# Second block's attention: stacked parts of queries and keys, split products, transposed results

## The chip, the cores and the metric

The kernel runs on one core of one Trainium2 chip. The metric is device time in microseconds (us), the median of three runs.

## The reference, cut to what matters

A two-stage network over 256 latent and 256 context tokens of width 1024. The stage that changes is the mixer of the second block's first layer. Its input is normed and modulated; three projections give queries, keys and values for 8 heads of 64 features, and the other half of the mixer (a long convolution, here called the hyena part) takes three more. Queries and keys are normed per head and scaled by a gain. Latent queries attend to a window of latent keys (a bias table `nabias` holds the window, with a large negative number outside) and to all context keys; context queries attend to context keys only:

```
q = rms_norm(q) * q_gain ;  k = rms_norm(k) * k_gain
latent:  s = q k^T / 8 + bias  (256 latent keys) ,  q k_ctx^T / 8  (256 context keys)
context: s = q k_ctx^T / 8     (256 context keys)
out = softmax(s) v            (per head; then side by side, times even_out, added to the stream)
```

## The kernel before, in words

Tokens stand in two segments of 256 (segment 0 latent, segment 1 context), each as two tiles of 128. Most products are done in three parts of a narrower 32-bit type (`F32R`): an operand is held as a high part H and a rest L, and `mm3` (lines 171 to 174) does H·H, H·L and L·H. `cut` (L145 to L151) makes the parts of a weight load of 128x1024: ScalarE (ACT) casts H, VectorE (DVE) subtracts for L. `split` (L176) does the same for activations. Plain `F32` products are issued in two pieces each.

The stage stands in lines 902 to 1060. Lines 912 to 931 make queries, keys and values token by token, six groups of two token tiles, 48 products of 512 columns each; queries and keys are normed and turned by four transposes per token tile into `qT` and `kT`, two heads on 128 partitions. `att2(qt, hb)` (L936 to L968) does one tile of 128 queries for four heads. Per head: one F32 score product with 64 rows (L946 or L952), for latent queries the bias is added on DVE (L947) and the other half copied by ACT (L948), DVE takes the row maximum (L956), ACT the exponential and its sum (L957), two or four transposes through the two `tp` banks and an ACT copy (L960) turn the weights, and two or four F32 products with 64 columns (L962) give the output with tokens on partitions; DVE divides by the sum (L965, L966). `heads(qt)` (L1021) later transposes and splits the result into `yH`, `yL`.

The order that the code writes: lines 1027 to 1037 alternate the hyena part's 12 `conv` products (24 products of 512 columns, then one ACT and two DVE instructions, L973 to L978) with six of the eight `att2` jobs; `spectrum(0)` (L981) comes behind the first of the last four convs, `signal(0)` (L1006) and `heads(0)`, `heads(1)` follow; then `out_proj` of segment 0 (L1059), between whose eight output tiles `rest()` puts `spectrum(1)`, the jobs 6 and 7, `heads(2)`, `heads(3)` and `signal(1)`, and then `out_proj` of segment 1.

The code's order is a priority: a planner (the tile framework) fixes each engine's order ahead of time from it and from its own estimate of when an instruction is ready, so that products of a later conv fill TensorE while an attention step waits. Tiles with one tag share a fixed number of buffers, and a new one waits until an old one is done with. Weight loads go through SP's queue; the bias tiles (L944, 16 loads of 128 KB) are issued by GpSimd (POOL), which does nothing else in this stage.

Of the kernel before, what the change touches and what calls it, by code (L numbers as in the profile page):

```python
# [10 lines left out]
F32 = mybir.dt.float32  # L11
# [62 lines left out]
def trace(tc, A, dbg=None):  # L74
# [32 lines left out]
    # ---------------------------------------------------------------- constants  # L107
# [20 lines left out]
    # ---------------------------------------------------------------- weights  # L128
# [4 lines left out]
    def queued(inst, prev):  # L133
        """Issues inst behind prev on their engine."""
# [10 lines left out]
    def cut(raw):  # L145
        """A load as its parts."""
# [6 lines left out]
    class Feed:  # L153
        """Weights in the order of their use, from the i-th load on."""
# [25 lines left out]
    # ---------------------------------------------------------------- 1/sqrt of small tiles  # L180
# [20 lines left out]
    # ---------------------------------------------------------------- modulation vectors  # L201
# [53 lines left out]
    def pump(k):  # L255
        """Emits k units behind other work: they fill what it leaves of the vector engine."""
# [36 lines left out]
    # ---------------------------------------------------------------- work put between products  # L293
# [12 lines left out]
    # ---------------------------------------------------------------- norms (features on partitions)  # L306
# [56 lines left out]
    class TwoNorms(Norm):  # L363
        """A norm with gain g, and a second norm of its result, both from sums over x: with
        v = mean(x^2) + eps, the second one's mean square + eps is (mean((x g)^2) + eps v) / v."""
# [47 lines left out]
    # ---------------------------------------------------------------- SwiGLU  # L413
# [9 lines left out]
    def up(w_gu, f, sub, hH, hL, tags):  # L423
        """One tile of hidden features of the segments in sub."""
# [22 lines left out]
    def ahead(pools, w_gu, seg, out):  # L447
        """The first tiles of hidden features of one segment, ahead of their FFN."""
# [6 lines left out]
    def ffn_steps(hp, nslot, w_gu, w_dn, keys, gate_ch, segs, norms, lead=0, done=None, pre=None):  # L455
        """One SwiGLU as steps: a tile of hidden features, or a tile of output features, each.
        With two segments the second product goes in groups of hidden tiles; the first `lead` tiles,
        and the last group of the second product, are done for one segment after the other, so that
        the norms around it overlap with products. pre: hidden tiles of the second segment at hand."""
# [442 lines left out]
    with ExitStack() as st:  # L902
# [9 lines left out]
        for i, (n, tiles) in enumerate(((0, lat), (1, lat), (0, ctx_), (1, ctx_), (2, ctx_), (2, lat))):  # L912
            out = proj_tm("even_qkv", n, tiles, ("mm", "mm") if i % 2 == 0 else ("sc", "sc"))
            tick(4)
            for ps, tt in zip(out, tiles):
                if n == 2:
                    act.copy(vt[tt], ps)
                    continue
# [114 lines left out]
        for c in range(4):  # L1033
# [3 lines left out]
            if 4 + c < 6:  # L1037
                att2(*jobs[4 + c])
# [385 lines left out]
```

## Time and profile before

| | |
|---|---|
| median of three runs | 2448.03 us (2446.39 to 2449.99) |
| the profiled execution | span 2448.3 us from first to last instruction; the page gives no other time for it |
| TensorE busy (PE) | 2409.3 us, 98% |
| DVE busy | 1690.1 us, 69% |
| ACT busy | 1011.4 us, 41% |
| POOL busy | 12.6 us |
| mean granted TensorE clock | 0.993 |

Busy times of PE count pipelined products up to a modelled end, so neighbours overlap; what one product costs in a dense stretch is read from start to start.

### The profile page before, as it was taken

The numbers are of one execution on the slowest core, as the hardware profiler recorded it, in microseconds if no ns is written. First come the engines' busy times: TensorE is split into PE (matmuls) and PEld (weight loads), VectorE is DVE, ScalarE is ACT, GpSimd is POOL, SyncE is SP. The second block draws the span as 40 slices with busy tenths as digits, with TensorE's granted clock in tenths as the row PEclk, the third lists the DMA queues.
The fourth block names the chain that finished last, engine by engine and source line by source line (L and its number), as shares of the span: only waits on it lengthen the run. The fifth ranks groups of instructions, "written<-read, shape, count | busy, mean of one in ns | idle before, by whom it ended". The sixth has DMA issues, their size and how long they took to land.

```text
span 2448.3 us, 38829 instructions
## 1 busy us (share of the span) xinstructions
PE 2409.3 (98%) x15624; PEld 2158.4 (88%) x15624; DVE 1690.1 (69%) x2957; ACT 1011.4 (41%) x1532; POOL 12.6 (1%) x27
## 2 busy tenths in 40 slices
PE   7999999999999999999999999999999999999999
PEld 4999889999998888777988888988888999999999
DVE  6889986666999588557875655886455775555554
ACT  4444575444332235555632222632222553334442
POOL 0000000000000000000000000000000000000000
PEclk8999999999999999999999999999999999999999
DMA  8887864565765455421463434564445543324554
GB/s 307 322 307 250 311 212 167 203 212 196 241 210 186 146 198 185 137 67 42 160 219 131 153 137 145 183 218 169 173 162 182 192 133 105 104 86 147 190 183 145
DMA packets 124372, 441.72 MB, mean 180 GB/s; under 512 B 13952, under 2 KB 18176, under 8 KB 124064
## 3 DMA queue, kind: packets, MB, share of 16 engines
q1 hardware_dynamic: 122928, 435.25, 51.4%
q0 software_dynamic: 1120, 3.80, 0.5%
q8 instruction: 122, 2.00, 0.3%
q14 instruction: 58, 0.48, 0.1%
q10 hardware_dynamic: 144, 0.19, 0.0%
HBM read 438.14 MB, written 1.05 MB: 179 GB/s over the span
## 4 chain that ended last, share of the span: by engine, by line
PE 90%; DVE 5%; DMA 2%; ACT 1%; issue 1%; SPq 0%; DVEq 0%; ACTq 0%
PE mm L172 15%; PE mm L173 15%; PE mm L174 15%; PE sc L174 13%; PE sc L173 13%; PE sc L172 13%; DVE wL L150 2%; DMA mraw<-in_wada_dram 1%; PE tp L574 1%; PE sm L962 1%; DVE mjunk L270 1%; PE tp L1150 1%; ACT wH L149 1%; PE sc L673 1%; DMA raw<-in_wada_sc_dram 0%
## 5 line engine op out<-in xcount | busy, mean ns | idle before, releaser
L149 ACT CAST wH<-wraw 128x1024 fp32r<-128x1024 f32 x596 | 624.6, 1049 | 1067.3 <-PE mm L173 416.3
L150 DVE TENSOR_TENSOR wL<-wraw,wH 128x1024 fp32r<-128x1024 f32 x596 | 728.0, 1223 | 396.8 <-ACT wH L149 385.3
L172 PE MATMUL mm<-yH,wH 128*128 128x256 f32 (+1 forms) x1744 | 561.9, 322 | 7.4 <-ACT wH L149 3.8
L174 PE MATMUL mm<-yH,wL 128*128 128x256 f32 (+1 forms) x1744 | 558.9, 320 | 3.6 <-DVE wL L150 3.5
L173 PE MATMUL mm<-yL,wH 128*128 128x256 f32 (+1 forms) x1744 | 560.0, 321 | 0.4 <-DVE yL L701 0.3
L174 PE MATMUL sc<-yH,wL 128*128 128x256 f32 (+1 forms) x1168 | 375.7, 322 | 2.2 <-DVE wL L150 2.2
L172 PE MATMUL sc<-yH,wH 128*128 128x256 f32 (+1 forms) x1168 | 376.5, 322 | 1.4 <-ACT yH L177 0.8
L173 PE MATMUL sc<-yL,wH 128*128 128x256 f32 (+1 forms) x1168 | 376.3, 322 | 0.0
L172 PEld LDWEIGHTS mm<-yH,wH 128*128 128x128 f32 x1744 | 330.6, 190 | 39.3 <-ACT wH L149 6.4
L174 PEld LDWEIGHTS mm<-yH,wL 128*128 128x128 f32 x1744 | 330.8, 190 | 29.0 <-DVE wL L150 4.5
L173 PEld LDWEIGHTS mm<-yL,wH 128*128 128x128 f32 x1744 | 330.6, 190 | 25.1 <-DVE yL L701 1.0
L270 DVE SCALAR_TENSOR_TENSOR mjunk<-mraw,crow_c 128x1024 bf16<-128x1024 f32 x200 | 244.1, 1220 | 23.8 <-DMA mraw<-in_wada_dram 16.9
L174 PEld LDWEIGHTS sc<-yH,wL 128*128 128x128 f32 x1168 | 221.3, 190 | 20.7 <-DVE wL L150 2.9
L172 PEld LDWEIGHTS sc<-yH,wH 128*128 128x128 f32 x1168 | 221.4, 190 | 19.6 <-ACT wH L149 1.0
L173 PEld LDWEIGHTS sc<-yL,wH 128*128 128x128 f32 x1168 | 221.6, 190 | 17.6
L174 PE MATMUL sc<-hH,wL 128*128 128x256 f32 (+1 forms) x640 | 192.9, 301 | 1.3 <-DVE wL L150 1.3
L172 PE MATMUL sc<-hH,wH 128*128 128x256 f32 (+1 forms) x640 | 194.1, 303 | 0.0
L172 PE MATMUL mm<-hH,wH 128*128 128x256 f32 (+1 forms) x640 | 194.0, 303 | 0.0
L173 PE MATMUL mm<-hL,wH 128*128 128x256 f32 (+1 forms) x640 | 193.9, 303 | 0.0
L173 PE MATMUL sc<-hL,wH 128*128 128x256 f32 (+1 forms) x640 | 193.5, 302 | 0.0
L174 PE MATMUL mm<-hH,wL 128*128 128x256 f32 (+1 forms) x640 | 192.9, 301 | 0.0
L270 DVE SCALAR_TENSOR_TENSOR mjunk<-mraw,crow_c_ctx 128x1024 bf16<-128x1024 f32 x112 | 136.8, 1222 | 4.8 <-ACT crow_c_ctx L224 2.8
(366 smaller groups left out, 3279.4 us busy)
## 6 DMA issues: line engine op xcount, KB each, us to landing
mraw<-in_wmod_dram SPq DMA_DIRECT2D x144, 512.0 KB, 4.6
wraw<-in_fa_gu_dram SPq DMA_DIRECT2D x114, 512.0 KB, 3.6
wraw<-in_fb_gu_dram SPq DMA_DIRECT2D x94, 512.0 KB, 3.3
wraw<-in_w_gu_dram SPq DMA_DIRECT2D x88, 512.0 KB, 3.7
wraw<-in_fa_dn_dram SPq DMA_DIRECT2D x60, 512.0 KB, 3.5
mraw<-in_wada_dram SPq DMA_DIRECT2D x56, 512.0 KB, 5.4
wraw<-in_fb_dn_dram SPq DMA_DIRECT2D x52, 512.0 KB, 3.3
wraw<-in_w_dn_dram SPq DMA_DIRECT2D x44, 512.0 KB, 4.0
```

Of the source, the lines that this page charges most:

```text
L149: act.copy(H, raw)
L150: vec.tensor_tensor(L, raw, f32(H), op=OP.subtract)
L172: pe.matmul(ps, aH, bH, start=start, stop=False)
L173: pe.matmul(ps, aH, bL, start=False, stop=False)
L174: pe.matmul(ps, aL, bH, start=False, stop=stop)
L270: queued(vec.scalar_tensor_tensor(junk, raw, 1.0, row_of(c), op0=OP.mult, op1=OP.mult, accum_out=mod[key][:, ch * 8 + j:ch * 8 + j + 1]), ...
L574: pe.transpose(pt[:, j * P:j * P + P], src(j), ident)
L673: pe.matmul(scp[j], csil[:, k:k + 1], raw[:, j * 512:j * 512 + 512], start=k == 0, stop=k == ND - 1)
L962: pe.matmul(po[:, (h % 4) * 64:(h % 4) * 64 + 64], pT[:, i, :], vt[kt][:, h * 64:h * 64 + 64], start=i == 0, stop=i == n - 1)
L1150: pe.matmul(ps[:, c], kT[:, j, jt * P:jt * P + P], qT[:, j, :], start=j == 0, stop=j == 1)
```

## The change

- Queries and keys stay token-major after their norm (`qkn`); the 32 transposes that turned them move into `att2_open(hp)`, once per pair of heads: eight transposes into both `tp` banks, then for each of the two heads H and L of the query (gain and 1/8 folded in) on the two halves of 128 partitions (`qq`), H of the key on both halves (`kH`), L of the key on one half with zeros on the other (`kL`), and H and L of the values side by side (`vv`; the subtraction on POOL).
- A score is two F32R products of 128 rows: `qq` with `kH`, `qq` with `kL`.
- `att2(h, seg)` does one head for both query tiles of a segment. For segment 1 the maximum and the exponential read the bank directly. The weights are divided by their sum before the transposes, on POOL; behind the transposes they are split into H (ACT) and L (DVE).
- The output has features on partitions: `vv` is the stationary operand, H and L of the weights are the moving ones (256 columns), and the two halves of the result are added (ACT copy, DVE add). `heads` has no transposes any more.
- Order: pairs of heads, segment 0 then 1, two (head, segment) steps between two convs; 14 of 16 steps stand ahead of the last four convs, the last two (heads 6 and 7 of segment 1) in `rest()`, ahead of `spectrum(1)`.
- Buffers: `spectrum` now takes its four work tiles from the two buffers of `a2pH` and the two of `a2pL`; `hyx0` takes the buffer of the token-major queries; `hy_b` has one buffer instead of two.

The diff also drops comments, which is left out here, as is the body of the old `att2`, which stands above.

```diff
@@ -902,70 +902,104 @@
     with ExitStack() as st:
         mp = pool("mix2", stack=st)
         wk = pool("mix2w", 2, stack=st)
-        hyx0 = tl(mp, [P, 4, 512], F32, "hyx0")
         hyz = tl(mp, [P, 4, 512], F32, "hyz")
         dft = tl(mp, [P, 8, P], F32, "dft")
         nc.sync.dma_start(dft, A["dft"].rearrange("p (n q) -> p n q", n=8))
-        qkT = [tl(mp, [P, 4, 512], F32, f"qk2T{i}") for i in range(2)]
-        vt = [tl(mp, [P, 512], F32, f"v2_{tt}") for tt in range(4)]
+        qkn = [tl(mp, [P, 4, 512], F32, f"qk2n{i}", 1) for i in range(2)]
+        vt = tl(mp, [P, 4, 512], F32, "v2")
+        pos = tl(mp, [P, 4, 512], F32, "at2")
         lat, ctx_ = (0, 1), (2, 3)
         for i, (n, tiles) in enumerate(((0, lat), (1, lat), (0, ctx_), (1, ctx_), (2, ctx_), (2, lat))):
             out = proj_tm("even_qkv", n, tiles, ("mm", "mm") if i % 2 == 0 else ("sc", "sc"))
             tick(4)
             for ps, tt in zip(out, tiles):
                 if n == 2:
-                    act.copy(vt[tt], ps)
+                    act.copy(vt[:, tt, :], ps)
                     continue
                 sq = tl(tpool, [P, 512], F32, "sg", 2)
                 act.activation(sq, ps, AF.Square)
                 ss = tl(spool, [P, 8], F32, "qss")
                 vec.tensor_reduce(ss, sq.rearrange("p (h e) -> p h e", h=8), AX, OP.add)
                 rs = mean_rsqrt(ss, 8, 64)
-                qn = tl(tpool, [P, 512], F32, "hf", 2)
-                vec.tensor_tensor(qn.rearrange("p (h e) -> p h e", h=8),
+                vec.tensor_tensor(qkn[n][:, tt, :].rearrange("p (h e) -> p h e", h=8),
                                   ps.rearrange("p (h e) -> p h e", h=8),
                                   rs.rearrange("p (h o) -> p h o", o=1).to_broadcast([P, 8, 64]), op=OP.mult)
-                tk = slice(tt * P, tt * P + P)
-                gcol = V("q_gain" if n == 0 else "k_gain")
-                transpose4(lambda j: qn[:, j * P:j * P + P],
-                           lambda pt: act.activation(qkT[n][:, :, tk], pt, AF.Identity, scale=gcol))
-        qT, kT = qkT
-        pos = [tl(mp, [P, 512], F32, f"at2_{qt}") for qt in range(4)]
-        rsum = tl(mp, [P, 4, 8], F32, "rsum2")
-        def att2(qt, hb):
-            po = bank("sm", [P, T])
-            for h in range(hb * 4, hb * 4 + 4):
-                rows = slice((h % 2) * 64, (h % 2) * 64 + 64)
-                qs = qT[rows, h // 2, qt * P:qt * P + P]
+        qg8 = tl(mp, [P, 1], F32, "qg8")
+        vec.tensor_scalar(qg8, V("q_gain"), 0.125, None, op0=OP.mult)
+        halves = (slice(0, 64), slice(64, P))
+        kL = [tl(mp, [P, 512], F32R, f"kL{e}") for e in range(2)]
+        for e in range(2):
+            vec.memset(f32(kL[e][halves[1 - e], :]), 0.0)
+            act.copy(kL[e][halves[1 - e], :], f32(kL[e][halves[1 - e], :]))
+        def att2_open(hp):
+            out = []
+            qt, kt = bank("tp"), bank("tp")
+            for n, pt in enumerate((qt, kt)):
+                for tt in range(4):
+                    pe.transpose(pt[:, tt * P:tt * P + P], qkn[n][:, tt, hp * P:hp * P + P], ident)
+            for e in range(2):
+                own, other = halves[e], halves[1 - e]
+                gq, gk = qg8[own, :], V("k_gain")[own, :]
+                qq = tl(wk, [P, 512], F32R, "qq", 2)
+                kH = tl(wk, [P, 512], F32R, "kH", 2)
+                act.activation(qq[own, :], qt[own, :], AF.Identity, scale=gq)
+                vec.scalar_tensor_tensor(qq[other, :], qt[own, :], gq, f32(qq[own, :]), op0=OP.mult, op1=OP.subtract)
+                act.activation(kH[own, :], kt[own, :], AF.Identity, scale=gk)
+                act.copy(kH[other, :], f32(kH[own, :]))
+                vec.scalar_tensor_tensor(kL[e][own, :], kt[own, :], gk, f32(kH[own, :]), op0=OP.mult, op1=OP.subtract)
+                h = 2 * hp + e
+                vv = tl(wk, [P, 4, 2, 64], F32R, "vv", 2)
+                src = vt[:, :, h * 64:h * 64 + 64]
+                act.copy(vv[:, :, e, :], src)
+                nc.gpsimd.tensor_tensor(vv[:, :, 1 - e, :], src, f32(vv[:, :, e, :]), op=OP.subtract)
+                out.append((qq, kH, kL[e], vv))
+            return out
+        def att2(h, seg, parts):
+            qq, kH, kL, vv = parts
+            nk, k0 = (512, 0) if seg == 0 else (T, T)
+            n = nk // P
+            pH = tl(wk, [P, 4, T], F32R, "a2pH", 2)
+            pL = tl(wk, [P, 4, T], F32R, "a2pL", 2)
+            for i in range(2):
+                qt = 2 * seg + i
+                tk = slice(qt * P, qt * P + P)
                 s = tl(wk, [P, 512], F32, "a2s", 4)
...
+                ps = bank("sc", [P, nk])
+                pe.matmul(ps, qq[:, tk], kH[:, k0:], start=True, stop=False)
+                pe.matmul(ps, qq[:, tk], kL[:, k0:], start=False, stop=True)
+                if seg == 0:
                     bt = tl(tpool, [P, T], F32, "hn", 3)
                     nc.gpsimd.dma_start(bt, A["nabias"][h, qt])
+                    vec.tensor_tensor(s[:, :T], ps[:, :T], bt, op=OP.add)
+                    act.copy(s[:, T:], ps[:, T:])
+                raw = s if seg == 0 else ps
                 nmx = tl(spool, [P, 1], F32, "nmx")
+                vec.tensor_reduce(nmx, raw[:, :nk], AX, OP.max, negate=True)
+                rsum = tl(spool, [P, 1], F32, "rsum2")
+                act.activation(s[:, :nk], raw[:, :nk], AF.Exp, bias=nmx, accum_out=rsum)
+                rin = tl(spool, [P, 1], F32, "sm_rin1")
+                vec.reciprocal(rin, rsum)
+                nc.gpsimd.tensor_scalar(s[:, :nk], s[:, :nk], rin, None, op0=OP.mult)
+                o = slice(i * P, i * P + P)
+                transpose4(lambda j: s[:, j * P:j * P + P], lambda pt: split(pH[:, :n, o], pL[:, :n, o], pt), n)
+            po = bank("sm", [P, T])
+            for j in range(n):
+                for x in (pH, pL):
+                    pe.matmul(po, vv[:, k0 // P + j, :, :], x[:, j, :], start=j == 0 and x is pH,
+                              stop=j == n - 1 and x is pL)
+            own, other = (slice(0, 64), slice(64, P)) if h % 2 == 0 else (slice(64, P), slice(0, 64))
+            low = tl(tpool, [P, T], F32, "sq", 4)
+            act.copy(low[own, :], po[other, :])
+            vec.tensor_tensor(pos[own, h // 2, seg * T:seg * T + T], po[own, :], low[own, :], op=OP.add)
         def conv(n, dst):
             ps = bank("mm")
@@ -979,16 +1013,16 @@
                                      op0=OP.mult, op1=OP.add)
         def spectrum(s):
-            """Transform of z, and its product with the filter's."""
-            zt = tl(wk, [P, 2, 512], F32, "zt", 1)
+            zt = tl(wk, [P, 2, 512], F32, "a2pH", 2)
             for par in range(2):
                 tk = slice(s * T + par, s * T + T, 2)
                 transpose4(lambda j: hyz[:, j, tk],
                            lambda pt: act.copy(zt[:, par, :].rearrange("p (n q) -> p n q", n=4), pt))
-            zr = tl(wk, [P, 2, 512], F32, "zr", 1)
-            zi = tl(wk, [P, 2, 512], F32, "zi", 1)
+            zr = tl(wk, [P, 2, 512], F32, "a2pL", 2)
+            zi = tl(wk, [P, 2, 512], F32, "a2pL", 2)
             half_spectra(dft, zt, zt, zr, zi, ("mm", "mm"))
-            yr = tl(wk, [P, 2, 512], F32, "yr", 1)
+            yr = tl(wk, [P, 2, 512], F32, "a2pH", 2)
             vec.tensor_tensor(yr, zr, specA, op=OP.mult)
             for i in range(2):
                 u = tl(tpool, [P, 512], F32, "sg", 2)
@@ -1018,39 +1052,45 @@
                 vec.tensor_tensor(o, o, hyx0[:, c, sl], op=OP.mult)
                 split(yH[:, 4 + c, sl], yL[:, 4 + c, sl], o)
-        def heads(qt):
-            tk = slice(qt * P, qt * P + P)
-            transpose4(lambda j: pos[qt][:, j * P:j * P + P], lambda pt: split(yH[:, :4, tk], yL[:, :4, tk], pt))
+        def heads(s):
+            sl = slice(s * T, s * T + T)
+            split(yH[:, :4, sl], yL[:, :4, sl], pos[:, :, sl])
         hyfeed = Feed("even_hy", 0)
-        jobs = [(qt, hb) for qt in range(4) for hb in range(2)]
+        todo = [(2 * hp + e, seg) for hp in range(4) for seg in range(2) for e in range(2)]
+        held = {}
+        def attend(n):
+            for _ in range(n):
+                h, seg = todo.pop(0)
+                if h % 2 == 0 and seg == 0:
+                    held[h // 2] = att2_open(h // 2)
+                att2(h, seg, held[h // 2][h % 2])
         for c in range(4):
             conv(4 + c, hyz[:, c, :])
-            att2(*jobs[c])
-            b = tl(wk, [P, 512], F32, "hy_b", 2)
+            attend(2)
+            b = tl(wk, [P, 512], F32, "hy_b", 1)
             conv(8 + c, b)
             vec.tensor_tensor(hyz[:, c, :], b, hyz[:, c, :], op=OP.mult)
+            if c < 3:
+                attend(2)
+        hyx0 = tl(mp, [P, 4, 512], F32, "qk2n0", 1)
         for c in range(4):
             conv(c, hyx0[:, c, :])
             if c == 0:
                 Y = spectrum(0)
-            if 4 + c < 6:
-                att2(*jobs[4 + c])
         signal(0, Y)
         heads(0)
-        heads(1)
         def rest():
-            """What the second segment lacks, between the products of the first."""
+            for _ in range(2):
+                attend(1)
+                yield
             Y = spectrum(1)
             yield
-            att2(*jobs[6])
-            yield
-            att2(*jobs[7])
-            yield
-            heads(2)
-            yield
-            heads(3)
+            heads(1)
             yield
             signal(1, Y)
             yield
```

## Rows read from the trace of the kernel before

**Rows 1.** The page: engines over the whole span, and the chain that ended last.

```profile
PE 2409.3 (98%) x15624; PEld 2158.4 (88%) x15624; DVE 1690.1 (69%) x2957; ACT 1011.4 (41%) x1532; POOL 12.6 (1%) x27
...
PE 90%; DVE 5%; DMA 2%; ACT 1%; issue 1%; SPq 0%; DVEq 0%; ACTq 0%
```

**Rows 2.** Windows of the stage: stretch, length, busy time (instructions) per engine, clock, DMA.

```profile
948.80:1009.50 60.70, 60.00 (x273) 47.97 (x272) 45.06 (x139) 32.96 (x42) 1.64 (x3) 1.00 0.54 181
1015.40:1097.90 82.50, 81.63 (x417) 59.82 (x417) 42.00 (x68) 40.85 (x82) 6.95 (x13) 1.00 0.23 73
1097.90:1132.20 34.30, 32.94 (x170) 24.09 (x168) 25.16 (x39) 18.78 (x46) 0.00 (x0) 1.00 0.13 47
1132.20:1178.00 45.80, 44.91 (x315) 38.19 (x316) 38.05 (x73) 23.35 (x57) 0.00 (x0) 1.00 0.23 77
```

**Rows 3.** Lines by shape, 936 to 1260 us, PE: the scores (busy, mean ns).

```profile
L946 PE MATMUL sc<-qk2T,qk2T 64*128 64x512 f32 x32 | 13.5, 641 | 0.9 <-ACT a2s L948 0.9
L952 PE MATMUL sc<-qk2T,qk2T 64*128 64x256 f32 x32 | 9.1, 428 | 0.0
```

**Rows 4.** Timeline of PE, 1015 to 1139 us: start, length, what.

```profile
1015.44 1.13 PE L946 MATMUL sc<-qk2T,qk2T 64*128 64x512 f32 x4
...
1090.65 1.07 PE L962 MATMUL sm<-v,a2pT 128*128 128x64 f32 x8
1091.53 0.47 PE L172 MATMUL mm<-yH,wH 128*128 128x512 f32 x1
...
1092.07 0.40 PE L174 MATMUL mm<-yH,wL 128*128 128x512 f32 x1
1092.31 0.39 PE L172 MATMUL mm<-yH,wH 128*128 128x512 f32 x1
...
1097.90 1.11 PE L574 MATMUL tp<-ident,hyz 128*128 128x128 f32 x8
...
1129.46 0.38 PE L1012 MATMUL mm<-dft,zt 128*128 128x128 f32 x2
...
1138.36 0.28 PE L172 MATMUL sc<-yH,wH 128*128 128x256 f32 x1
1138.48 0.28 PE L173 MATMUL sc<-yL,wH 128*128 128x256 f32 x1
```

**Rows 5.** Lines by shape, 936 to 1260 us, ACT.

```profile
L957 ACT ACTIVATE a2s<-a2s,nmx 128x512 f32<-128x512 f32 x16 | 11.5, 720 | 2.6 <-DVE nmx L956 2.6
L960 ACT COPY a2pT<-tp 128x512 f32<-128x512 f32 x16 | 9.4, 585 | 10.2 <-PE tp L574 9.6
L957 ACT ACTIVATE a2s<-a2s,nmx 128x256 f32<-128x256 f32 x16 | 8.1, 506 | 3.1 <-DVE nmx L956 3.1
L957 ACT ACTIVATION_READ_ACCUMULATOR a2s<-a2s,nmx 128x1 f32 x32 | 6.1, 189 | 0.0
L948 ACT ACTIVATE a2s<-sc 128x256 f32<-128x256 f32 x16 | 5.5, 371 | 6.4 <-DVE a2s L947 6.4
L931 ACT ACTIVATE qk2T<-tp,vecs 128x512 f32<-128x512 f32 x8 | 5.5, 690 | 3.6 <-PE tp L574 3.6
```

**Rows 6.** The same view, DVE and POOL.

```profile
L956 DVE TENSOR_REDUCE nmx<-a2s 128x1 f32<-128x512 f32 x16 | 10.6, 681 | 5.1 <-ACT a2s L948 5.1
L947 DVE SCALAR_TENSOR_TENSOR a2s<-sc,hn 128x256 f32<-128x256 f32 x16 | 6.7, 419 | 3.4 <-PE sc L946 3.2
L976 DVE SCALAR_TENSOR_TENSOR hyx<-mm,vecs,hyx 128x510 f32<-128x510 f32 x4 | 3.0, 742 | 0.0
L178 DVE TENSOR_TENSOR yL<-tp,yH 128x512 fp32r<-128x512 f32 x4 | 2.7, 684 | 0.0
```

**Rows 7.** Lines over the whole span, POOL: its one large elementwise instruction.

```profile
L743 POOL TENSOR_SCALAR_AFFINE_SELECT wst<-wst 128x1024 f32<-128x1024 f32 x1 | 1.1, 1087 | 9.6 <-DMA wst<-in_wsT_dram 9.6
```

**Rows 8.** Timeline of DVE, 1100 to 1119 us: inside and at the end of the first spectrum.

```profile
1109.50 1.29 DVE L995 TENSOR_TENSOR sg<-zi,specB 128x512 f32<-128x512 f32 x2
...
1117.46 0.69 DVE L1003 TENSOR_TENSOR yr<-zi 128x512 f32<-128x512 f32 x1
```

More of the change, by code (lines that the diff above doesn't have):

```diff
@@ L941, in att2 @@
+        def att2(h, seg, parts):
[7 more added lines that the diff above has]
+                tk = slice(qt * P, qt * P + P)
                 s = tl(wk, [P, 512], F32, "a2s", 4)
-                if qt < 2:
+                ps = bank("sc", [P, nk])
+                pe.matmul(ps, qq[:, tk], kH[:, k0:], start=True, stop=False)
+                pe.matmul(ps, qq[:, tk], kL[:, k0:], start=False, stop=True)
+                if seg == 0:
@@ L943, in att2 @@
                     bt = tl(tpool, [P, T], F32, "hn", 3)
                     nc.gpsimd.dma_start(bt, A["nabias"][h, qt])
-                    ps = bank("sc")
-                    pe.matmul(ps, qs, kT[rows, h // 2, :], start=True, stop=True)
-                    vec.scalar_tensor_tensor(s[:, :T], ps[:, :T], 0.125, bt, op0=OP.mult, op1=OP.add)
-                    act.activation(s[:, T:], ps[:, T:], AF.Copy, scale=0.125)
-                    nk, kts = 512, (0, 1, 2, 3)
-                else:
-                    ps = bank("sc", [P, T])
-                    pe.matmul(ps, qs, kT[rows, h // 2, T:], start=True, stop=True)
-                    act.activation(s[:, :T], ps, AF.Copy, scale=0.125)
-                    nk, kts = T, (2, 3)
@@ L955, in att2 @@
-                nmx = tl(spool, [P, 1], F32, "nmx")
-                vec.tensor_reduce(nmx, s[:, :nk], AX, OP.max, negate=True)
-                act.activation(s[:, :nk], s[:, :nk], AF.Exp, bias=nmx, accum_out=rsum[:, qt, h:h + 1])
-                pT = tl(wk, [P, 4, P], F32, "a2pT", 2)
-                n = len(kts)
-                transpose4(lambda j: s[:, j * P:j * P + P], lambda pt: act.copy(pT[:, :n, :], pt), n)
-                for i, kt in enumerate(kts):
-                    pe.matmul(po[:, (h % 4) * 64:(h % 4) * 64 + 64], pT[:, i, :], vt[kt][:, h * 64:h * 64 + 64],
-                              start=i == 0, stop=i == n - 1)
@@ L964, in att2 @@
-            rin = tl(spool, [P, 4], F32, "sm_rin4")
-            vec.reciprocal(rin, rsum[:, qt, hb * 4:hb * 4 + 4])
-            vec.tensor_tensor(pos[qt][:, hb * T:hb * T + T].rearrange("p (h e) -> p h e", h=4),
-                              po.rearrange("p (h e) -> p h e", h=4),
-                              rin.rearrange("p (h o) -> p h o", o=1).to_broadcast([P, 4, 64]), op=OP.mult)
+                    vec.tensor_tensor(s[:, :T], ps[:, :T], bt, op=OP.add)
+                    act.copy(s[:, T:], ps[:, T:])
```

## Prediction, made before the changed kernel was run

> **What bounds the kernel now.** I read the page first: PE is busy 98% of the span and 90% of the chain that ended last is PE [rows 1]. So time is saved where PE is given less to do, as long as nothing else becomes late. Next come the windows of the stage [rows 2]: the q, k, v projections (948.8 to 1009.5), the stretch from the first score product to the last product of the hyena part's z (1015.4 to 1097.9, "the first part"), the rest up to the output product, and the output product of segment 0 with what is put between its tiles. PE is full in each, at the full clock of 2.4 GHz (1.00). DVE and ACT are about half used in the first part (42.0 and 40.9 of 82.5 us), but DVE is at 38.1 of 45.8 in the last window. The reader should see that PE work taken out is worth its time only while these two stay below PE. The lines by shape and the timeline give prices.
>
> **PE, part by part.** Pitches from start to start [rows 4]: a 512-column product 0.235 us (1092.07 to 1092.31), a 256-column one 0.12, a transpose 0.14 (eight in 1.11), one head's eight value pieces 0.88, so 0.11 each.
> - Projections: 32 transposes of queries and keys leave this window: -4.5 us. They reappear in the first part as 4 openings of 8.
> - First part before: 7 convs x 24 x 0.235 = 39.5, score pieces 13.5 [rows 3], 64 transposes 9.0, 128 value pieces 14.1: 76.1. The window took 82.5, a factor 1.08 for switching between kinds.
> - First part after: the same convs 39.5; openings 4.5; 32 score products of 512 columns for the 16 latent (head, tile) steps 7.5; 24 of 256 columns for 12 context ones 2.9; 88 transposes 12.3; 88 value products of 256 columns 10.6: 77.3, times 1.08 = 84. This stretch does not shrink, since it now also holds six heads of segment 1 and the openings.
> - Behind it: jobs 4 and 5 are gone from the next stretch: 16 score pieces (half of the 9.1 of [rows 3], 4.6), 16 transposes 2.2, 32 value pieces 3.5, with 8 output transposes 1.1: -11.4.
> - The last window loses the same 11.4 for jobs 6 and 7 with their output transposes and gets 3.1 (two heads: 8 score products 1.0, 8 transposes 1.1, 8 value products 1.0): -8.3.
>
> All together PE has about 22.7 us less: -4.5 + 1.5 - 11.4 - 8.3.
>
> **ACT in the first part.** Before: 40.9, of which attention is 11.5 + 9.4 + 5.5 + 16 x 0.19 = 29.4 [rows 5]; 11.5 is left for convs and casts. After: a latent step is 0.72 + 0.19 + 0.37 + 0.585 = 1.87, times 16 = 29.8; a context step 0.51 + 0.19 + 0.37 = 1.07, times 12 = 12.8; 14 copies of half the output 5.2; per head in an opening 0.69 + 0.69 (as L931 [rows 5]), a copy between the halves 0.59 and the value cast 0.37, 8 x 2.34 = 18.7. Sum 66.5 + 11.5 = 78.
>
> **DVE in the first part.** Before 42.0; attention was 10.6 + 6.7 + about 2.4 = 19.7 [rows 6], so 22.3 stays. After: a latent step 0.42 + 0.68 + 0.2 + 0.68 = 1.98, times 16 = 31.7; a context step 0.41 + 0.2 + 0.42 = 1.03, times 12 = 12.4; 14 additions 5.9; 16 subtractions in the openings at the conv's 0.74 [rows 6], 11.8. Sum 61.8 + 22.3 = 84. Two instructions of 0.69 in a row take 1.29 [rows 8], 0.09 less than their durations, so some 124 more instructions cost about 74 when they stand dense. I take 78, the middle.
>
> **POOL** has only DMA issues here. It gets 32 multiplications and 8 subtractions; the trace holds one large elementwise instruction, 1.09 us for 1024 elements [rows 7], so 0.55 and 0.27 by length. Bounds: hidden (0), or 1.09 each on the path. Its bias DMAs, unchanged in number, now stand in one queue with multiplications that wait for a DVE reciprocal; three buffers cover that, and if they don't, a latent step waits for its bias. The transposes wait for POOL, and behind them in PE's fixed order stand conv products. SP's queue gets nothing; weight casts stand behind more ACT and DVE work, and if late, conv products wait.
>
> **The sum.** In the first part PE 84, DVE 78, ACT 78: three engines that feed each other in a chain, where before only PE was full. 84 is the lower bound. The upper one is a serial reading: `att2_open` holds both `tp` banks and the double buffers of `qq`, `kH`, `vv`, so a pair begins when the one before has let go: 5.8 for the opening (1.1 of transposes and two times 2.34 of ACT), about 10 for the first latent chain (score to addition 7.5 and 13 hand-offs of an estimated 0.2), 5.6 for three more at ACT's 1.87, 5 for the tail of segment 1: 26.4, three times, and 21 for the last pair, which leaves its segment 1 to later: 100; with POOL at its upper price 107. I take 94, 12% above PE's 84, nearer to the lower end because conv work fills gaps on all three. In the spare 10 us PE runs the next convs ahead.
>
> The first spectrum starts when this part ends. Before, from its transposes at 1097.9 to its last DVE instruction at 1118.1 [rows 4, 8], it took 20.2; PE then needed until 1129.5 for convs and jobs 4 and 5 before `signal(0)` [rows 4]. Now its buffers are the attention's, so it cannot start sooner, and `signal(0)` starts at 1015.4 + 94 + 20.2 = 1129.6: nothing gained there; the 11.4 us of PE are eaten by the spectrum's chain. In the last window DVE's work is unchanged (two heads' context steps 4.1 + 0.8 and a split 1.2 against eight maxima, four divisions and two splits, about 6), so 38.1 is its floor against PE's 45.8 - 8.3 = 37.5; with both full I take 42: -4. Total: -4.5 + 0 - 4 = -8.5 on the profiled 2448.3, which is 0.3 above the median: **2439.5 us**. What a measurement of this kernel can tell from no change is about 0.2%, 4.9 us.
>
> **Rivals.**
> 1. PE stays the only bound and all 22.7 us are seen: 2426. For it: DVE and ACT sit below PE in each window; the planner fills gaps well today (1.4 us of 34.3 idle [rows 2]). Against: three engines within 10% of each other. Chance 0.15.
> 2. POOL and DVE hinder each other. In this kernel POOL never works beside DVE, so no row speaks against it. 14 of the 15 us of POOL's new work (about 1.07 ns an element [rows 7]) lie in the first part; if DVE stands still for that long, it has 92, and with the same 12% the part takes 103: +0.6, 2448.6. The Trainium skill has such a rule in "SBUF — State Buffer", section "SBUF: two separate sides": GpSimd and a DVE instruction with two SBUF inputs take a shared port pair in turns, and the loser waits for the whole instruction. Chance 0.24, no change.
> 3. Slower: the shared buffers make pairs serial. Place: `tp`, `qq`, `vv` between pairs, and `a2pH`/`a2pL` between attention and spectrum. Price: a first part of 107 puts `signal(0)` 13 later, and in the last window heads 6 and 7 wait for `signal(0)`, `spectrum(1)` for them, which takes the 4 back: -4.5 + 13 = +8.6, 2457. It decides from a first part of about 102 on, where the sum is zero. For it: before, spectrum had its own tiles and the query and key tiles were whole. Against: score products let `qq` go early. Chance 0.21.
> That the change doesn't make the score products cheaper is unlikely, and gets no chance of its own: two of 512 columns at 0.235 are 0.47 per head, where the F32 ones took 13.5 us for 16, 0.84 each [rows 3], and 0.57 each at best, side by side in two halves of the rows (four pieces in 1.13 [rows 4]).
>
> **How the numbers follow.** My case (2432 to 2443) has 0.40, rival 1 0.15: faster 0.55. Rival 2 is no change, 0.24; rival 3 slower, 0.21. The range runs from near rival 1 to near rival 3, 2427 to 2455, and leaves out about 0.2; the forecast's own range is 2432 to 2443.
>
> **What would show it.** Right: the projections' window about 4 us shorter; the first part 90 to 98 us with ACT and DVE near 80% or more; PE idle before `signal(0)` with DVE in the spectrum; value products at 0.12. Wrong: a first part at 84 and PE full (rival 1); durations of two-input DVE instructions grown next to POOL's (rival 2); openings that wait for the pair before, with PE, DVE and ACT idle at once (rival 3). A granted clock below 1.00 in the spectrum's stretch, which no window shows today, would add to it.

## The result: slower, and the profile after

The changed kernel takes 2467.2 us (median; 2464.24 to 2469.64) against 2449.01 us for the kernel before in the same comparison: a ratio of 1.0074, interval 1.0062 to 1.0085. The forecast was 2439.5, its range 2427 to 2455. The profiled executions are 2467.9 and 2448.3 us long. The page of the changed kernel, engines over the whole span, answers to [rows 1]:

```profile
PE 2402.0 (97%) x15512; PEld 2162.1 (88%) x15512; DVE 1726.5 (70%) x3038; ACT 1026.7 (42%) x1556; POOL 64.6 (3%) x67
```

PE was given less to do, as planned, and the kernel is longer. So waits are to be looked for, and the windows say where. The four stretches are those of [rows 2], cut at the same events in both kernels: the projections; the first score product to the first transpose of the hyena part's z ("first part"); from there to `signal(0)`; from there to the first product of the norm that closes segment 0 (L343). Columns are as in [rows 2].

```profile
948.80:1005.00 56.20, 56.20 (x243) 45.61 (x242) 45.51 (x141) 28.34 (x35) 1.64 (x3) 1.00 0.59 197
1015.60:1122.80 107.20, 87.21 (x428) 66.87 (x429) 77.61 (x156) 70.48 (x156) 51.33 (x47) 0.91 0.19 59
1122.80:1148.70 25.90, 24.09 (x98) 17.19 (x97) 19.70 (x26) 7.79 (x11) 0.00 (x0) 0.97 0.12 41
1148.70:1208.00 59.30, 50.79 (x344) 46.14 (x343) 44.78 (x86) 25.59 (x49) 5.13 (x4) 0.88 0.23 76
```

The last two stretches of the kernel before, cut in this way, are:

```profile
1097.90:1129.50 31.60, 31.02 (x154) 22.41 (x153) 23.46 (x37) 16.18 (x43) 0.00 (x0) 1.00 0.14 51
1129.50:1186.00 56.50, 54.83 (x398) 47.60 (x396) 45.39 (x88) 31.98 (x70) 0.00 (x0) 1.00 0.25 85
```

Nearly all of the loss stands in one place: the first part went from 82.5 to 107.2 us, the spectrum's stretch gave 5.7 back, the last one lost 2.8. In the first part PE is idle for 20 us, and the mean granted clock is 0.91, so PE ran some of it at the lower level, 1.2 GHz; before it was 1.00. The waits of the changed kernel between 1015 and 1125 us (who waits <- for whom: us in total, times, longest) name the cause:

```profile
PEld tp L574 <- POOL a2s L990: 20.8, 22, 2.6
ACT a2pH L177 <- PE tp L574: 19.8, 19, 2.2
DVE a2pL L178 <- ACT a2pH L177: 16.8, 20, 2.0
POOL a2s L990 <- DVE sm_rin L989: 15.2, 10, 3.8
PE tp L574 <- POOL a2s L990: 13.8, 19, 1.9
```

L990 is the division by the sum, a multiplication on POOL. The transposes of the weights wait for it (one stall can stand in both of PE's lines, so they are not to be added), and ACT and DVE, which split what the transposes give, wait for PE in turn. POOL itself waits for the reciprocal (L989): it is a link in a chain, not a full engine. The lines of POOL by shape, 1011.7 to 1215 us:

```profile
L990 POOL TENSOR_SCALAR a2s<-a2s,sm_rin 128x512 f32<-128x512 f32 x16 | 25.7, 1611 | 6.2 <-DVE sm_rin L989 5.0 <-ACT a2s L982 1.1
L990 POOL TENSOR_SCALAR a2s<-a2s,sm_rin 128x256 f32<-128x256 f32 x16 | 19.2, 1206 | 54.4 <-DVE sm_rin L989 51.7 <-PE sc L977 2.8
```

The reader is to see the means: 1.61 us for 512 elements and 1.21 for 256, where [rows 7] had 1.09 for 1024, for another instruction. The timeline shows the link at work (start, length, what, in brackets the idle time before it and who ended it):

```profile
1066.55 0.17 DVE L989 RECIPROCAL sm_rin<-rsum 128x1 f32<-128x1 f32 x1
...
1066.63 1.23 DVE L150 TENSOR_TENSOR wL<-wraw,wH 128x1024 fp32r<-128x1024 f32 x1
...
1066.88 1.76 POOL L990 TENSOR_SCALAR a2s<-a2s,sm_rin 128x256 f32<-128x256 f32 x1 [1.83 <-DVE sm_rin L989]
...
1068.70 0.44 PE L574 MATMUL tp<-ident,a2s 128*128 128x128 f32 x2 [0.94 <-POOL a2s L990]
...
1068.89 0.48 PE L173 MATMUL mm<-yL,wH 128*128 128x512 f32 x1
...
1070.71 0.92 POOL L990 TENSOR_SCALAR a2s<-a2s,sm_rin 128x256 f32<-128x256 f32 x1
```

The reciprocal ends at 1066.72; the transposes start at 1068.70, 0.06 after POOL has ended. The conv product at 1068.89 needs nothing of this, but it stands behind the transposes in PE's fixed order, and so it waits too.

### The profile page after: what moved, and what is told of

Its sections match the earlier page's. It is cut to its first block, busy times and chain, and to the rows that moved or that the text cites. A ratio compares the mean times of both kernels' runs of the same rounds, so it can differ in the third digit from the quotient of the medians.

```text
span 2467.9 us, 38788 instructions
## 1 busy us (share of the span) xinstructions
PE 2402.0 (97%) x15512; PEld 2162.1 (88%) x15512; DVE 1726.5 (70%) x3038; ACT 1026.7 (42%) x1556; POOL 64.6 (3%) x67
## 4 chain that ended last, share of the span: by engine, by line
PE 50%; DVE 2%; ACT 0%; issue 0%; POOL 0%; ACTq 0%; DVEq 0%; POOLq 0%
PE mm L172 8%; PE mm L173 8%; PE mm L174 8%; PE sc L174 8%; PE sc L173 8%; PE sc L172 8%; PE tp L1190 1%; DVE wL L150 0%; PE sm L174 0%; PE sm L173 0%; PE sm L172 0%; PE tp L574 0%; PE mm L1046 0%; ACT wH L149 0%; PE sm L343 0%
## 5 line engine op out<-in xcount | busy, mean ns | idle before, releaser
L150 DVE TENSOR_TENSOR wL<-wraw,wH 128x1024 fp32r<-128x1024 f32 x596 | 728.7, 1224 | 378.6 <-ACT wH L149 367.3
L172 PE MATMUL mm<-yH,wH 128*128 128x256 f32 (+1 forms) x1744 | 562.4, 323 | 8.0 <-ACT wH L149 3.8
L172 PE MATMUL sc<-yH,wH 128*128 128x256 f32 (+1 forms) x1168 | 378.8, 324 | 1.5 <-ACT a2s L987 1.4
L172 PEld LDWEIGHTS mm<-yH,wH 128*128 128x128 f32 x1744 | 332.0, 190 | 34.2 <-ACT yH L358 4.2
L172 PEld LDWEIGHTS sc<-yH,wH 128*128 128x128 f32 x1168 | 223.1, 191 | 20.1 <-ACT a2s L987 1.6
L172 PE MATMUL sc<-hH,wH 128*128 128x256 f32 (+1 forms) x640 | 194.0, 303 | 0.0
L172 PE MATMUL mm<-hH,wH 128*128 128x256 f32 (+1 forms) x640 | 193.9, 303 | 0.0
```

What stands on the lines that cost most here:

```text
L150: vec.tensor_tensor(L, raw, f32(H), op=OP.subtract)
L172: pe.matmul(ps, aH, bH, start=start, stop=False)
```

## The experiments

All are edits of the changed kernel. Ratios are to the kernel before, from the same comparison.

**The multiplication on DVE** (`e1_mul_dve`).

```diff
-                nc.gpsimd.tensor_scalar(s[:, :nk], s[:, :nk], rin, None, op0=OP.mult)
+                vec.tensor_scalar(s[:, :nk], s[:, :nk], rin, None, op0=OP.mult)
```

> Edit: the multiplication of the softmax weights by 1/sum runs on DVE instead of POOL. Theory A (the multiplication on POOL, 1.61 us for 512 and 1.21 for 256 columns, is what the transposes and behind them all of TensorE wait for): the first part goes from 107 us to 93-99, waits of TensorE on the multiplication below 10 us, total 2450-2458. Theory B (shared buffers make the steps serial): the first part stays within 3 us of 107, total 2462-2470. Theory C (DVE and ACT are simply full): total not below 2464, since DVE gets 28 more instructions there.

Measured: 2454.35 us, ratio 1.0031 (1.0019 to 1.0042). On DVE one multiplication takes 0.33 to 0.75 us. The first part:

```profile
1012.80:1109.60 96.80, 86.12 (x428) 67.03 (x429) 86.07 (x184) 69.45 (x156) 14.38 (x19) 0.93 0.20 66
```

It is 10.4 us shorter than with POOL, although DVE now has 86 us of work in it. Over the whole kernel, PE's products wait 3.3 us for the multiplication, where they waited 15.5 for POOL's.

**The multiplication taken out** (`e2_no_mul`).

```diff
-                nc.gpsimd.tensor_scalar(s[:, :nk], s[:, :nk], rin, None, op0=OP.mult)
```

> Edit: the multiplication by 1/sum is left out (the weights are not divided by their sum, everything else stands). A: the whole price of the step goes: first part 88-97, total 2444-2454. B: first part above 103, total above 2461. C: in between, 2455-2462, since only POOL work is taken away and POOL is at 51 of 111 us.

Measured: 2437.76 us, ratio 0.9961 (0.9946 to 0.9976). Between the ratios of the two kernels, 1.0074 and 0.9961, lie 27.7 us: this one line costs more than the whole loss. The first part, the spectrum's stretch and the last one:

```profile
1009.90:1094.40 84.50, 80.36 (x431) 63.29 (x431) 74.75 (x155) 70.21 (x157) 12.52 (x19) 1.00 0.21 69
1094.40:1120.00 25.60, 24.06 (x96) 17.77 (x96) 20.74 (x27) 7.21 (x10) 0.00 (x0) 0.94 0.18 62
1120.00:1176.60 56.60, 49.54 (x344) 45.42 (x343) 44.76 (x86) 25.38 (x49) 0.00 (x0) 0.91 0.24 83
```

84.5 us at a clock of 1.00 is close to the 84 that the prediction counted as PE's floor, with DVE at 75 and ACT at 70 us beside it.

**The spectrum in tiles of its own** (`e4_spec_bufs`): rival 3's shared `a2pH` and `a2pL`. The keys' token-major tile and the values' tile, both read to the end by then, hold the spectrum.

```diff
-        vt = tl(mp, [P, 4, 512], F32, "v2")
+        vt = tl(mp, [P, 4, 512], F32, "v2", 1)
...
-            zt = tl(wk, [P, 2, 512], F32, "a2pH", 2)
+            zy = tl(mp, [P, 4, 512], F32, "qk2n1", 1)
+            zt, yr = zy[:, :2, :], zy[:, 2:, :]
...
-            zr = tl(wk, [P, 2, 512], F32, "a2pL", 2)
-            zi = tl(wk, [P, 2, 512], F32, "a2pL", 2)
-            half_spectra(dft, zt, zt, zr, zi, ("mm", "mm"))
-            yr = tl(wk, [P, 2, 512], F32, "a2pH", 2)
+            zz = tl(mp, [P, 4, 512], F32, "v2", 1)
+            zr, zi = zz[:, :2, :], zz[:, 2:, :]
+            half_spectra(dft, zt, zt, zr, zi, ("mm", "mm"))
```

> Edit: spectrum takes its four work tiles from the buffers of the token-major keys and of the values (free after the last opening) instead of those of the attention's split weights; POOL keeps its multiplication. A: the first part stays at 107; only the steps of heads 6 and 7 of segment 1 come sooner, total 2461-2467. B: spectrum no longer waits for the last attention step nor that step for signal(0): signal(0) starts 5-15 us sooner, total 2450-2460.

Measured: 2465.47 us, ratio 1.0075 (1.006 to 1.0091). The first part is still 105.9 us (1015.7 to 1121.6), and `signal(0)` comes 25.9 after it. These buffers hold nothing up.

**The multiplication twice** (`e5_mul_twice`).

```diff
                 nc.gpsimd.tensor_scalar(s[:, :nk], s[:, :nk], rin, None, op0=OP.mult)
+                nc.gpsimd.tensor_scalar(s[:, :nk], s[:, :nk], 1.0, None, op0=OP.mult)
```

> Edit: a second multiplication on POOL, by 1.0, behind the first. A: POOL's chain grows by another 1.6 or 0.9 us per step, 28 steps in the first part, of which half or more is seen: total 2485-2510. B: hidden behind waits for buffers, total 2466-2474. C: hidden likewise, 2466-2476.

Measured: 2485.91 us, ratio 1.0157 (1.0142 to 1.0172), 20.3 us above the changed kernel by the ratios. The first part is 126.7 us at a granted clock of 0.81. POOL's lines by shape, 1011 to 1210 us:

```profile
L990 POOL TENSOR_SCALAR a2s<-a2s,sm_rin 128x512 f32<-128x512 f32 x16 | 25.0, 1565 | 5.2 <-DVE sm_rin L989 5.0
L991 POOL TENSOR_SCALAR a2s<-a2s 128x512 f32<-128x512 f32 x16 | 24.2, 1515 | 0.8
L990 POOL TENSOR_SCALAR a2s<-a2s,sm_rin 128x256 f32<-128x256 f32 x16 | 18.6, 1168 | 44.0 <-DVE sm_rin L989 44.0
L991 POOL TENSOR_SCALAR a2s<-a2s 128x256 f32<-128x256 f32 x16 | 14.5, 912 | 0.4
```

The second multiplication has 38.7 us of its own, and the time grows by 20: the chain has some slack, but not enough for the second copy. The granted clock fell too, from 0.91 to 0.81, so not all of the 20 us need be waiting. POOL is busy for 84.9 of the 126.7 us, so it isn't full even here.

**POOL as busy as ever, but nobody waits for it** (`f1_mul_aside`).

```diff
-                nc.gpsimd.tensor_scalar(s[:, :nk], s[:, :nk], rin, None, op0=OP.mult)
+                jk = tl(wk, [P, 512], BF16, "jk", 1)
+                nc.gpsimd.tensor_scalar(jk[:, :nk], s[:, :nk], rin, None, op0=OP.mult)
```

> Edit: POOL multiplies as in the changed kernel, but into a tile that nobody reads; the transposes take the weights not divided by their sum (the division is left out of the output). A (what costs is that the transposes wait for POOL): as without the multiplication, 2437-2443, first part 84-88, though POOL is as busy as in the changed kernel. Rival 2 (POOL beside DVE slows DVE, or the queue of bias loads behind POOL's work is late): 2452-2467.

Measured: 2440.85 us, ratio 0.997 (0.996 to 0.998). POOL's lines, 1011 to 1150 us:

```profile
L991 POOL TENSOR_SCALAR jk<-a2s,sm_rin 128x512 bf16<-128x512 f32 x16 | 25.6, 1602 | 8.8 <-DVE sm_rin L989 8.2
L991 POOL TENSOR_SCALAR jk<-a2s,sm_rin 128x256 bf16<-128x256 f32 x16 | 17.9, 1118 | 39.1 <-DVE sm_rin L989 36.6 <-ACT a2pH L177 1.5
```

And the first part in its window:

```profile
1013.70:1098.10 84.40, 80.17 (x431) 63.12 (x431) 74.67 (x155) 70.29 (x157) 49.80 (x47) 1.00 0.22 70
```

POOL does 49.8 us of work beside DVE, and the first part is 84.4 as with none of it. So the loss is the wait, not the load on a shared resource: rival 2's mechanism costs this stage nothing that can be measured.

**The division behind the products** (`e6_div_behind`). It computes all that is asked: the output, with queries along its columns, is multiplied by 1/sum, which two F32 products with an identity spread over the partitions, into the other half of the bank.

```diff
+            rins = []
...
-                nc.gpsimd.tensor_scalar(s[:, :nk], s[:, :nk], rin, None, op0=OP.mult)
+                rins.append(rin)
...
-            po = bank("sm", [P, T])
+            pb = bank("sm")
+            po, rb = pb[:, :T], pb[:, T:]
...
+            for i in range(2):
+                pe.matmul(rb[:, i * P:i * P + P], rins[i].to_broadcast([P, P]), ident, start=True, stop=True)
             low = tl(tpool, [P, T], F32, "sq", 4)
             act.copy(low[own, :], po[other, :])
-            vec.tensor_tensor(pos[own, h // 2, seg * T:seg * T + T], po[own, :], low[own, :], op=OP.add)
+            vec.tensor_tensor(low[own, :], po[own, :], low[own, :], op=OP.add)
+            vec.tensor_tensor(pos[own, h // 2, seg * T:seg * T + T], low[own, :], rb[own, :], op=OP.mult)
```

> Edit: no multiplication ahead of the transposes; 1/sum is spread over the partitions by two products per head and segment behind the value products, and DVE multiplies the output by it. A (what costs is a slow step in the chain ahead of the transposes, not the division as such): near the run without the division (2437.8), plus at most 7 us of TensorE (64 pieces of 0.11) and some DVE: 2438-2446, first part 84-91. Rival D (ACT, DVE and TensorE are so full that each added instruction costs its length): 2446-2454, as with the multiplication on DVE (2454.4).

Measured: 2447.13 us, ratio 0.9994 (0.9985 to 1.0003): above the 2438 to 2446 of reading A, and inside the range of rival D, for which each added instruction costs its length. The first part is 90.1 us (1015.0 to 1105.1), 5.6 more than without a division. It has 50 more PE instructions than `e2_no_mul`, an estimated 5.5 us at 0.11 each, and 6.3 us more of DVE. Either would account for the 5.6 us; which of the two does is not shown.

**The same, with the transforms in other banks** (`e7_sc_banks`).

```diff
-            half_spectra(dft, zt, zt, zr, zi, ("mm", "mm"))
+            half_spectra(dft, zt, zt, zr, zi, ("sc", "sc"))
```

> Edit: as e6, and the spectrum's transforms use the two sc banks instead of the two mm banks. E (from the first spectrum transpose to signal(0) it is 26 us because the transforms hold the convs' banks and TensorE has nothing else to do): that stretch falls to 20-22, total 4-6 below e6. Rival (it is the chain of the spectrum on DVE): the stretch stays above 24, total within 2 of e6.

Measured: 2440.01 us, ratio 0.9963 (0.9949 to 0.9977). It asks why the spectrum's stretch took 25.9 us after, where 20.2 were forecast. PE's timeline of the changed kernel in that stretch:

```profile
1125.99 2.11 PE L584 MATMUL mm<-a2pH,dft 128*128 128x512 f32 x4
1128.78 1.13 PE L584 MATMUL mm<-a2pH,dft 128*128 128x512 f32 x2 [0.67 <-ACT hf L586]
1130.10 1.13 PE L584 MATMUL mm<-a2pH,dft 128*128 128x512 f32 x2 [0.20 <-DVE a2pL L589]
1131.90 0.50 PE L172 MATMUL mm<-yH,wH 128*128 128x512 f32 x1 [0.67 <-ACT hf L586]
```

The transforms (L584) sit in the two `mm` banks, which the conv products need; between them PE is idle, for 1.5 us in all, and the convs come only behind the last of them: 72 products, 16.9 us at 0.235 each. With the transforms in `sc`, the timeline of `e7_sc_banks` reads:

```profile
1106.16 2.12 PE L584 MATMUL sc<-a2pH,dft 128*128 128x512 f32 x4
...
1108.58 0.40 PE L172 MATMUL mm<-yH,wH 128*128 128x512 f32 x1
...
1109.05 1.03 PE L584 MATMUL sc<-a2pH,dft 128*128 128x512 f32 x2
...
1110.15 0.40 PE L172 MATMUL mm<-yH,wH 128*128 128x512 f32 x1
1110.39 1.02 PE L584 MATMUL sc<-a2pH,dft 128*128 128x512 f32 x2
```

Convs now stand between the transforms, and the stretch fell to 19.6 us from the 26.1 of `e6_div_behind`:

```profile
1102.80:1122.40 19.60, 18.44 (x84) 13.39 (x82) 17.91 (x25) 9.27 (x13) 0.00 (x0) 1.00 0.08 27
```

The idle time is the smaller part of this gain. The lines by shape count the conv products that are left for the stretch; L172 is one in three of them, first `e6_div_behind` (1105.1 to 1131.2 us), then `e7_sc_banks` (1102.8 to 1122.4):

```profile
L172 PE MATMUL mm<-yH,wH 128*128 128x512 f32 x24 | 9.6, 399 | 0.7 <-ACT hf L586 0.7
...
L172 PE MATMUL mm<-yH,wH 128*128 128x512 f32 x16 | 6.3, 395 | 0.0
```

Of all three lines 72 products became 50. The others now run in the first part, which holds 202 conv products instead of 181 and is no longer for it (89.8 us against 90.1): with `mm` left to the convs, they fill gaps there.

**Own tiles for the spectrum, and `spectrum(1)` earlier** (`e9_own_bufs`): `e6_div_behind` with the tiles of `e4_spec_bufs` and the last two attention steps behind `spectrum(1)`.

```diff
         def rest():
+            Y = spectrum(1)
+            yield
             for _ in range(2):
                 attend(1)
                 yield
-            Y = spectrum(1)
-            yield
```

> Edit: as e6, and spectrum has work tiles of its own (the buffers of the token-major keys and of the values), so spectrum(1) is put ahead of the last two attention steps again, as it was before. B (buffers shared by spectrum and attention hold the last window): signal(0) to the norm behind segment 0 (57-59 us) falls by 4-9, total 4-9 below e6. Rival: the window is filled by DVE, total within 2 of e6.

Measured: 2444.9 us, ratio 0.9989 (0.998 to 0.9997). The last stretch is 52.9 us (1127.3 to 1180.2) against 54.4. The step is 2 us where 4 to 9 were expected, and the intervals of the two kernels overlap.

**Both together** (`e8_both`): the edits of `e7_sc_banks` and `e9_own_bufs`.

> Edit: e7 and e9 together. B and E: the gains add, 8-14 below e6, so 2426-2434, below the kernel before by 14-22. Rivals: within 3 of e6.

Measured: 2443.27 us, ratio 0.9983 (0.9974 to 0.9992): a miss. The spectrum's stretch is short (19.6 us), but the last one has grown to 57.5. The gains don't add up.

**1/sum spread by one transpose per tile** (`f2_div_turned`): `e7_sc_banks` with one transpose where an F32 product stood.

```diff
-                pe.matmul(rb[:, i * P:i * P + P], rins[i].to_broadcast([P, P]), ident, start=True, stop=True)
+                pe.transpose(rb[:, i * P:i * P + P], rins[i].to_broadcast([P, P]), ident)
```

> Edit: as the run with the division behind the products and the sc banks, but 1/sum is spread by one transpose per tile instead of a product of two pieces: 32 x (0.22 - 0.14) = 2.6 us of TensorE less. If TensorE bounds the first part: 1-3 us below 2440; if DVE does: within 1.5 us.

Measured: 2444.79 us, ratio 0.9985 (0.9976 to 0.9994): a miss, no gain over `e7_sc_banks`. The first part is 92.3 us, not shorter than 89.8, but it holds 218 conv products, 16 more. PE then has too few left for the spectrum's stretch and waits for DVE at its end (PE, 1117 to 1126 us):

```profile
1120.17 0.28 PE L978 MATMUL sc<-kL,qq 128*128 128x256 f32 x1
1125.26 1.01 PE L1051 MATMUL mm<-dft,a2pH 128*128 128x128 f32 x3 [4.80 <-DVE qk2n L1017]
```

L1051 is the first product of `signal(0)`. So the stretch stays at 19.4 us, the length of the spectrum's chain, and the products that ran ahead gain nothing.

**That, with the spectrum in tiles of its own** (`f3_turned_bufs`), the order of `rest()` as in the change.

> Edit: as f2, and spectrum with work tiles of its own (buffers of the token-major keys and of the values), the order of rest() left as in the changed kernel. B: the last window no longer waits for signal(0) to give up its buffers, 2-5 us below f2. Rival: within 1.5 us of f2.

Measured: 2445.64 us, ratio 0.9987 (0.9978 to 0.9996). The buffers make no difference here either.

**The best version again** (`g1_best_again`): `e7_sc_banks` timed again, unchanged.

> The kernel with the division behind the products and the transforms in the sc banks again, in more rounds. If its gain is real: 2437-2443, ratio to the kernel before 0.995-0.998, interval below 1. If it was the luck of few runs: 2443-2447, as its neighbours f2 and f3.

Measured: 2441.21 us, ratio 0.9975 (0.9966 to 0.9985). By the ratios it is 0.25% faster than the kernel before, about 6 us (the medians of this comparison, 2441.21 and 2444.94, are 3.7 apart), and about 24 us faster than the changed one.

## Why the prediction was wrong

**The step that failed** is POOL's multiplication, its price and its place. The price was "0.55 and 0.27 by length", from the row of another instruction [rows 7], with 1.09 as upper bound; it measured 1.61 and 1.21, above the bound for either length. And the 94 us chosen for the first part have no term for the wait of the transposes. With that wait the first part took 107.2 us, without it 84.5 (`e2_no_mul`) and 84.4 (`f1_mul_aside`). That conv products cannot pass a late transpose was written down ("behind them in PE's fixed order stand conv products"); with the price so small it was given no weight. The text also gave 100 us for a serial reading and 107 "with POOL at its upper price", and chose 94 because conv work would fill the gaps. That it came out at 107.2 is chance: with the multiplication gone, nothing of the serial reading is left.

What the price alone is worth is not shown. On DVE the multiplication took 0.33 to 0.75 us, near the price assumed, and the first part was still 96.8 us; but there DVE had 11.3 us more work than in `e2_no_mul`.

Every stretch against the forecast, from the profiles. The projections and the first opening run up to the first score, which came 1.0 us earlier than before, counted from the norm's closing product ahead of the stage (L329, 912.1 and 913.3 us).

| | forecast | after | without the multiplication |
|---|---|---|---|
| up to the first score | -4.5 | -1.0 | -1.1 |
| first part | +11.5 | +24.7 | +2.0 |
| up to `signal(0)` | -11.4 | -5.7 | -6.0 |
| up to the norm's end, segment 0 | -4 | +2.8 | +0.1 |
| sum (the prediction rounds it to -8.5) | -8.4 | +20.8 | -5.0 |

Behind the last row the changed kernel is another 2.4 us shorter, and the one without the multiplication 3.0, for which no step had been named. The first two rows belong together: the forecast counted all four openings in the first part, and in the trace the first one stands ahead of the first score. So 7.0 were forecast for both and 23.7 came, 0.9 without the multiplication.

- **The projections** end 3.6 us earlier on the trace and 4.8 counted from the stage's start: -4.5 was right.
- **PE's count** came out right by luck. Its floor of 84 was measured as 84.5 and 84.4 as soon as nobody waited for POOL, and the value products come every 0.12 us. But its terms don't hold. The first of the last four convs stands ahead of the spectrum, so it belongs to the first part too. The lines by shape of the kernel before, 1015.4 to 1097.9 us:

```profile
L172 PE MATMUL mm<-yH,wH 128*128 128x512 f32 x64 | 26.7, 417 | 0.0
L174 PE MATMUL mm<-yH,wL 128*128 128x512 f32 x65 | 26.4, 407 | 0.0
L173 PE MATMUL mm<-yL,wH 128*128 128x512 f32 x64 | 25.9, 404 | 0.0
```

These are 193 conv products, eight convs, where seven (168) were counted. At 0.235 us each they bring the sum from 76.1 to 82.0 of the 82.5 us, so next to nothing is left of the factor 1.08 "for switching between kinds". In `e2_no_mul` the first part holds 181 conv products, three openings and 81 value products, at the same pitches 78.3 us; PE is busy for 80.4 of the 84.5 and idle for 4.1. Over the whole span `e2_no_mul` has PE busy for 2390.6 us, 18.7 below before, where 22.7 were counted.
- **DVE and ACT** were forecast at 78 each in the first part and had 77.6 and 70.5. The factor of 12% on PE's floor for three engines that feed each other was not needed: 84.5 us hold 75 of DVE and 70 of ACT. The nearness of three engines, the argument against rival 1, costs nothing measurable here; one slow link in their chain does.
- **The spectrum's stretch** was forecast at 20.2 us because "PE runs the next convs ahead". It took 25.9, since none of the last three convs found a bank ahead of the transforms and all their 72 products stood behind them; `e7_sc_banks` shows 19.6 with banks for them. As the length of the spectrum's chain 20.2 was about right: `f2_div_turned`, where PE waits for it, has 19.4. Before, two attention jobs stood in this gap.
- **The last stretch** gained nothing instead of 4, even without the multiplication (56.6 against 56.5). There PE had 5.3 us less work (54.8 to 49.5) and as much more idle time; DVE, called the floor, is busy for 44.8. Neither is full, and the granted clock of 0.91 says that PE ran part of it at the lower level. The waits of `e2_no_mul` in it show a chain through DVE and ACT that PE used to cover:

```profile
PE mm L1045 <- DVE a2pH L1033: 2.6, 1, 2.6
PE mm L1045 <- DVE resid L419: 1.6, 1, 1.6
PE tp L574 <- ACT a2s L987: 1.4, 1, 1.4
PE mm L1045 <- DVE sq L1049: 0.7, 1, 0.7
```

Without the multiplication the kernel stands at 2437.8 us, close to the forecast of 2439.5. That is partly chance: the first part was 6 us better than forecast, the two stretches behind it 9.5 worse, and 3.0 came from behind the stage. Another 4.4 us of its shorter profile lie ahead of the stage, where the two kernels do the same.

**The rivals.** Rival 1 (PE alone bounds, 2426) holds for the first part, nearly, once the multiplication is gone, not for the stretches behind. Rival 2 (POOL and DVE hinder each other) falls with `f1_mul_aside` as a cause of the loss. What it describes is there. The multiplication of 256 elements took 0.92 us beside a DVE instruction that reads one of its inputs from a bank (L1012), and 1.76 beside DVE's cut of 1024 elements (L150), which reads two tiles, and it ended 0.78 us after the cut; the cut itself has a mean of 1.22 us in the changed kernel and in the one without the multiplication alike. The Trainium skill, "SBUF — State Buffer", section "SBUF: two separate sides", has GpSimd and a DVE instruction with two SBUF inputs take their port in turns; the trace agrees for POOL, which waits there, and once for DVE. Its product of two tiles (L1075) took 0.67 to 0.68 us three times, and 1.00 us where it began just behind a multiplication on POOL (1027.15 to 1027.25 us):

```profile
1026.96 1.55 POOL L990 TENSOR_SCALAR a2s<-a2s,sm_rin 128x512 f32<-128x512 f32 x1
...
1027.18 1.00 DVE L1075 TENSOR_TENSOR hyz<-hy_b,hyz 128x512 f32<-128x512 f32 x1
```

It did not wait for the whole instruction, as that section and rival 2 have it: it ended 0.33 us ahead of POOL's, and in `f1_mul_aside` the same product began 0.99 us into a multiplication of 512 elements and took 0.68.

Rival 3 named the first part's length, 107, and the sign, but its place was wrong: of its buffers, `a2pH` and `a2pL` towards the spectrum are shown to be harmless (`e4_spec_bufs`, and `f3_turned_bufs` without POOL's wait), and the openings' `tp`, `qq` and `vv` do not keep the first part from 84.5 us.

**Left open.** Whether `e8_both`, `f2_div_turned` and `f3_turned_bufs` are really slower than `e7_sc_banks`: their medians are 3 to 6 us above it, but their intervals overlap with that of its repeat, `g1_best_again`. Each edit gives the planner another fixed order (218 conv products in the first part of the two last-named, 202 in the others), and no run separates that from the edit. How much of the first part's loss is the lower clock was not tried by itself. As an estimate: PE is busy there for 87.2 us with 428 instructions, and for 80.4 with 431 in `e2_no_mul`, so about 6.9 of the 22.7 us between the two are longer instructions, and 15.8 are idle time.

## What to carry to other kernels

An operation handed to an idle engine is free only if nothing in a fixed order waits for it; otherwise some or all of its length is on the path, and each product planned as filler behind the waiting instruction waits too. Price it by a row of that very instruction on that engine, or run it once as a side copy that nobody reads, as `f1_mul_aside` does: load and wait then come apart. A division by a row sum can move behind the products, and before counting on filler work, look which banks it needs. Count what a window holds from the trace's own counts: a factor that is left over, as the 1.08 here, may be work that was forgotten.

## What the runs showed of the hardware that was not expected

POOL's multiplication by a per-partition scalar or a constant took 1.52 us for 512 elements and 0.91 for 256 when it ran behind another of its kind (L991 of `e5_mul_twice`): about 2.4 ns for each further element, where the one instruction of [rows 7] took 1.09 us for 1024. DVE did the same operation in 0.33 to 0.75 us. A subtraction of two 256-element inputs on POOL took 0.73 us (L961 of the changed kernel, 732 ns on average), less than a multiplication with one. Its price cannot be read from the length alone.
